# A hybrid attention and recurrence layer on one core: q and k turned by VectorE and DRAM, the recurrence's output products moved into the second score run

## The chip, the core and the metric

The kernel runs on one core of a Trainium2 chip. Five engines work from instruction queues of their own: TensorE (PE in the profile; PEld are its weight loads), VectorE (DVE), ScalarE (ACT), GpSimd (POOL) and SyncE (SP), of which the last two only issue transfers here. The metric is the device time of one execution in microseconds.

## The reference

One layer of a decoder trunk, 512 tokens, 1024 channels, all in fp32. After an RMS norm one projection gives ten groups of columns: q, k, v and a gate of an attention branch (8 heads of 64), q, f, i and g of a gated recurrence (4 heads of 128), and two merge gates.

```python
xn = rmsnorm(h, norm_gain[i])
aq, ak, av, ag, bq, bf, bi, bg, gate_a, gate_b = jnp.split(xn @ w_in[i], split_pts, axis=-1)
qa = rmsnorm(heads(aq), q_norm_gain[i]); ka = rmsnorm(heads(ak), k_norm_gain[i])
ya = moba_attention(qa, ka, heads(av), rel_bias)          # causal, with a bias by distance
ya = (ya * silu(ag)) @ w_up_a[i]
yb = hgrn2_chunkwise(silu(bq), kb, bi, log_f)             # kb and log_f come from bf
yb = (rmsnorm(yb, hgrn_out_gain[i]) * silu(bg)) @ w_up_b[i]
merged = sigmoid(gate_a) * ya + sigmoid(gate_b) * yb
h = h + merged @ w_out[i]
h = h + (p[i] @ w_ple[i]) * sigmoid(h @ w_ple_gate[i])
```

## The kernel before

Every fp32 product is made of three reduced products: each operand is split into a high part (ACT, a copy that rounds) and a low part (DVE, the difference), lines 216 to 222, and `mm3` (line 278) sums high x high, high x low and low x high. Weights come through GpSimd's queue, are split two blocks ahead of their use and held in three buffers (`wh`, `wl`). One block is 24 matmuls of 512 columns. The names of the blocks in the profile are those of the projections: `aq` and `ak` (attention's q and k, with tokens on the partitions), `av`, `bi`, and, with channels on the partitions, `bf` and `bq` (recurrence), `ag` and `bg` (silu gates), `ga` and `gb` (merge gates), `ub` and `ua` (up projections), `h`, `pe`, `g`.

The order of PE's instructions is written out: the program keeps a clock of estimated microseconds (`now`, lines 100 to 135), the projections are issued in the order of `ORDER` (line 51), and generators that stand aside (`spawn`) are resumed when that clock passes what they last yielded. So `yield 14.0` in `qk_norm`, `PACE`, `HOP` and the like say between which projections their matmuls fall. The order on ACT, DVE and SP is made by a scheduler out of its own estimates; `held` (line 143) forbids it to put an instruction ahead of the projection issued last, `held_from` (line 149) does so some microseconds of the clock later, and `tc.high_priority` moves an instruction forward. Each queue runs strictly in its order on the chip.

Four parts matter for the change.

- `qk_norm` (line 703) copies the four banks of `aq` or `ak` out of PSUM into slots of the tile `pb` (128 x 9 x 512), squares and sums them, and multiplies each head by its factor. Then it turns each pair of heads, 128 channels, on PE: four transposes of 128x128 by the identity (line 726, `qtp`, `ktp`) into one bank, from which ACT and DVE make the scaled high and low part (line 221 and 222).
- `attention` (line 734) makes for each of four head pairs two score runs: the first over queries 0 to 383 (`s` of step 0), the second over queries 384 to 511 (step 1). Behind each run stands its softmax: DVE adds a bias read from the tile `bias` (line 778), ACT exponentiates and divides (780, 782), DVE turns 32x32 blocks (785), and sixteen small transfers on SP sort the blocks (796), from slots of `pb` to other slots of `pb`. After both runs of a pair `out_values` multiplies by v (`o`, line 809).
- The recurrence (lines 493 to 700) works on one head at a time. `hgrn_intra` multiplies blocks of a 128-token chunk against each other (`lpb`, `lpa`; operands `hx`), gathers the result in one score matrix `sc` (last by ACT, line 639), and turns its keys by 32x32 blocks on DVE and through DRAM (`turned_keys`, line 599; `hkt`, `there`). `hgrn_out` makes the chunk states (`hds`, `st`) and then, `HOP` microseconds of the clock later, the output products `hop`: four of `sc` with the values and three of the states with q, into a bank of the tag `g`. ACT squares the result (667), DVE multiplies it into the gate (670), turns and sums the squares (302, 304) and so on to the normalised, gated output.
- PSUM has three banks for projections (tag `mm`), two for the recurrence (`g`), three for attention (`a`), used in turn.

Of the kernel before, what the change touches and what calls it, by code (L numbers as in the profile page):

```python
# [11 lines left out]
F32 = mybir.dt.float32  # L12
R = mybir.dt.float32r
I32 = mybir.dt.int32
AF = mybir.ActivationFunctionType
# [6 lines left out]
NT = S // 128  # L22
# [6 lines left out]
LEVELS = (16, 8, 4, 2, 1)  # L29

STEPS = ((0, 1, 2), (3,))
PACE = (20.0, 21.0)

HP = 2.5
H0 = 8.0

HOP = 9.0

BESIDE = 30.0

# [23 lines left out]
def hybrid_layer_kernel(  # L64
# [68 lines left out]
    def cost(us):  # L133
        now[0] += us
# [36 lines left out]
            xr.append(t)  # L171


    pb = cst.tile([128, 9, 512], F32, name="pb")
    xfirst = pb[:, 0, 0:272]
    raw0 = unit("w", "wf0", shape=(128, 2, 512))
    A.preload_act_table_set("natural_log_exp_and_others")
# [304 lines left out]


    hg = {}

    runs = [1000]

    def beside_attention():
        seen, until = runs[0], now[0] + BESIDE
        if seen < 1000:  # L490
            yield lambda: runs[0] > seen or now[0] >= until
# [24 lines left out]
    def hgrn_intra(h):  # L516
# [50 lines left out]
        k16 = kq(16)  # L567
        yield HP
        yield from beside_attention()
        lpb = bank("g", f"lpb{h}").rearrange("p (l c t) -> p l c t", l=4, c=NT)  # L570
        big = lpb[:, 2:4].rearrange("p l c t -> p (l c t)").rearrange("p (c t) -> p c t", c=NT)
        lpa = bank("g", f"lpa{h}").rearrange("p (l c t) -> p l c t", l=4, c=NT)
# [49 lines left out]
            yield HP  # L622
        if not h:
            kd, kts = turned_keys()
        yield 6.0 if h else 8.0

        A.activation(cum, cum, AF.Exp)
        V.tensor_tensor(q[:, 128:], q[:, 128:], cum[:, 128:], op=OP.mult)
# [13 lines left out]
    def hgrn_out(h, vb, sbg):  # L642
        kb, q, cum, kd = hg[h][:4]
        hv = slice(h * 128, h * 128 + 128)
        dsp = bank("g", f"hds{h}")
        done.add(f"hds{h}")
        for c in range(3):
            PE.matmul(dsp[:, c * 128:c * 128 + 128], kd[:, c * 128:c * 128 + 128], vb[c][:, hv],
                      start=True, stop=True)
        cost(0.65)  # L650
        st = unit("st", f"st{h}", shape=(128, 3, 128))
        V.tensor_copy(st[:, 0], dsp[:, 0:128])
        for c in (1, 2):
            e = c * 128 + 127
            V.scalar_tensor_tensor(st[:, c], st[:, c - 1], cum[:, e:e + 1], dsp[:, c * 128:c * 128 + 128],
                                   op0=OP.mult, op1=OP.add)
        yield HOP
        op_ = bank("g", f"hop{h}")
        for c in range(NT):
            s_ = slice(c * 128, c * 128 + 128)  # L660
            PE.matmul(op_[:, s_], vb[c][:, hv], sc[:, c, :], start=True, stop=(c == 0))
            if c:
                PE.matmul(op_[:, s_], st[:, c - 1], q[:, s_], start=False, stop=True)
        cost(1.5)
        o = unit("YB", f"ho{h}")
        y = unit("N", f"hy{h}")
        A.activation(o, op_, AF.Square)
        gated = f"bg{h}" in done
        if gated:
            V.scalar_tensor_tensor(sbg[h], op_, ogain[:, h:h + 1], sbg[h], op0=OP.mult, op1=OP.mult)  # L670
        token_spread(y, token_factor(token_sums(o, y, 1.0 / 128)))
        if gated:
            V.tensor_tensor(sbg[h], sbg[h], y, op=OP.mult)
        else:
            V.scalar_tensor_tensor(o, op_, ogain[:, h:h + 1], y, op0=OP.mult, op1=OP.mult)
        hg[h] += (None if gated else o,)
# [23 lines left out]
            yield HP  # L700


    def qk_norm(name, banks, g, res):
        hs = [unit("A", f"{name}h{i}", R) for i in range(HPAIRS)]
        ls = [unit("A", f"{name}l{i}", R) for i in range(HPAIRS)]
        raws = []
        ss = cst.tile([128, NT, HEADS], F32, name=name + "ss")
        y = cst.tile([128, NT, HEADS], F32, name=name + "y")
        t_ = cst.tile([128, NT, HEADS], F32, name=name + "t")
        for t in range(NT):  # L710
            raw = pb[:, (0 if name == "q" else 4) + t]
            A.activation(raw, banks[t], AF.Copy)
            sq = pb[:, ((8, 4, 5) if name == "q" else (8, 0, 1))[t % 3]]
            A.activation(sq, raw, AF.Square)
            V.tensor_reduce(ss[:, t], sq.rearrange("p (h d) -> p h d", h=HEADS), axis=AX.X, op=OP.add)
            raws.append(raw)
        V.tensor_scalar(ss, ss, 1.0 / 64, None, op0=OP.mult)
        rsqrt(y, t_, ss)
        for t in range(NT):
            r3 = raws[t].rearrange("p (h d) -> p h d", h=HEADS)  # L720
            V.tensor_tensor(r3, r3, y[:, t, :, None].to_broadcast([128, HEADS, 64]), op=OP.mult)
        yield 14.0
        for i in range(HPAIRS):
            tp = bank("a", f"{name}tp{i}")
            for t in range(NT):
                PE.transpose(tp[:, t * 128:t * 128 + 128], raws[t][:, i * 128:i * 128 + 128], ident)
            cost(0.44)
            with tc.high_priority(offset=AHEAD):
                scale_split(hs[i], ls[i], tp, g)
            res.append((hs[i], ls[i]))  # L730
            yield 1.3
        done.add(name)

    def attention(qn, kn, va, sags, res):
# [84 lines left out]

        while not {"q", "k"} <= done:  # L820
            yield lambda: {"q", "k"} <= done
        yield 3.0
        runs[0] = 0
        NS = len(STEPS)
        steps = [(hp, i) for hp in range(HPAIRS) for i in range(NS)]
# [1 line left out]
        for n in range(len(steps) + 1):  # L827
# [15 lines left out]
                    yield lambda: f"ag{ho}" in done  # L843
                out_values(ho, [pts.pop(n - NS + i_) for i_ in range(NS)])
            if n < len(steps):
                pts[n] = sorted_groups(i, softmax(hp, i, [T[hp, 0], T[hp, 1]], where))
            runs[0] += 1
        runs[0] += 1000

# [242 lines left out]
```

## Time and profile before

| | |
|---|---|
| median of 3 runs | 459.85 us (459.64 to 460.42) |
| the profiled execution, its own time | 459.45 us |
| its span, first to last instruction | 457.7 us |
| granted TensorE clock | 1.000 |
| PE busy | 451.6 us, 99% of the span |
| VectorE busy | 300.0 us, 66% |
| ScalarE busy | 276.1 us, 60% |

Rows of the chain, of a timeline and of the waits give start and length in microseconds, then engine, line, the tile written and the tiles read (`hop<-sc,biv`), and how many instructions are merged. In brackets stands how long the engine was idle before, and what ended that. A chain is followed back from the last instruction to what released each step, so what stands in it lengthens the time.

### The profile page before, as it was taken

To read this page: it belongs to the slowest core of one execution; us is meant where nothing else is said; L and a number is where in the kernel's file an instruction comes from. 1 tells how busy PE (TensorE), PEld (TensorE's weight loads), DVE (VectorE), ACT (ScalarE), POOL (GpSimd) and SP (SyncE) were. 2 spreads that over 40 slices of the span, in tenths; PEclk is the share of its full clock that TensorE was granted. 3 is DMA by queue.
4 is the path that set the end of the run, shared out by engine and by line. 5 is a ranking of instruction groups with operands and counts; after the bars stand their busy time and mean duration, and the time that the engine had idled before them with its cause. 6 is when DMAs were issued, how large, how long until landed. Compare 5 with 4: busy or idle time off the path is not lost.

```text
span 457.7 us, 8117 instructions
## 1 busy us (share of the span) xinstructions
PE 451.6 (99%) x3094; PEld 374.5 (82%) x3094; DVE 300.0 (66%) x608; ACT 276.1 (60%) x532; POOL 38.6 (8%) x77
## 2 busy tenths in 40 slices
PE   9999999999999999999999999999999999999996
PEld 8888888788888788878887888878888888888886
DVE  5869493867899586959786835564569744544222
ACT  5957565747789597968887877784435433322201
POOL 1000100000000000010100000101210100000000
PEclk9999999999999999999999999999999999999999
DMA  7802434222123626152525154454631744220111
GB/s 255 318 1 94 137 109 156 93 93 78 62 94 107 181 82 197 46 172 80 170 79 166 57 178 124 145 155 138 231 98 46 233 153 139 92 107 32 46 47 46
DMA packets 26470, 55.30 MB, mean 121 GB/s; under 512 B 6720, under 2 KB 12608, under 8 KB 26432
## 3 DMA queue, kind: packets, MB, share of 16 engines
q0 software_dynamic: 9056, 32.51, 21.7%
q1 hardware_dynamic: 17232, 22.27, 15.8%
q8 instruction: 24, 0.39, 0.4%
q14 instruction: 14, 0.11, 0.1%
q10 hardware_dynamic: 144, 0.01, 0.0%
HBM read 46.65 MB, written 2.88 MB: 108 GB/s over the span
## 4 chain that ended last, share of the span: by engine, by line
PE 96%; ACT 2%; issue 1%; DVE 1%; DVEq 0%; ACTq 0%
PE g L282 10%; PE h L282 10%; PE ga L282 9%; PE gb L282 9%; PE bf L282 5%; PE bg L282 5%; PE ub L282 5%; PE av L412 5%; PE bq L282 5%; PE ua L282 5%; PE ag L282 5%; PE bi L412 4%; PE aq L412 4%; PE ak L412 4%; PE pe L282 2%; PE o L809 2%
## 5 line engine op out<-in xcount | busy, mean ns | idle before, releaser
L217 ACT ACTIVATE wh<-wf 128x1024 fp32r<-128x1024 f32 (+1 forms) x78 | 75.6, 970 | 90.2 <-issue 32.2
L218 DVE TENSOR_TENSOR wl<-wf,wh 128x1024 fp32r<-128x1024 f32 (+1 forms) x78 | 86.8, 1112 | 53.1 <-ACT wh L217 52.8
L256 POOL DMA_DIRECT2D wf<-in_w_tr_dram x30 | 15.9, 530 | 175.2 <-DVE wl L218 135.1
L282 PE MATMUL g<-hh,wh 128*128 128x512 f32 (+1 forms) x72 | 26.3, 365 | 0.0
L282 PE MATMUL g<-hl,wh 128*128 128x512 f32 (+1 forms) x72 | 26.3, 365 | 0.0
L282 PE MATMUL g<-hh,wl 128*128 128x512 f32 (+1 forms) x72 | 26.3, 365 | 0.0
L282 PE MATMUL ga<-xh,wh 128*128 128x512 f32 x64 | 25.4, 397 | 0.0
L282 PE MATMUL gb<-xh,wh 128*128 128x512 f32 x64 | 25.0, 391 | 0.0
L282 PE MATMUL ga<-xh,wl 128*128 128x512 f32 x64 | 24.9, 390 | 0.0
L282 PE MATMUL ga<-xl,wh 128*128 128x512 f32 x64 | 24.9, 390 | 0.0
L282 PE MATMUL gb<-xh,wl 128*128 128x512 f32 x64 | 24.9, 389 | 0.0
L282 PE MATMUL gb<-xl,wh 128*128 128x512 f32 x64 | 24.9, 389 | 0.0
L282 PE MATMUL h<-mh,wh 128*128 128x512 f32 x64 | 24.9, 389 | 0.0
L282 PE MATMUL h<-ml,wh 128*128 128x512 f32 x64 | 24.9, 389 | 0.0
L282 PE MATMUL h<-mh,wl 128*128 128x512 f32 x64 | 24.9, 389 | 0.0
L780 ACT ACTIVATE pb<-pb,ps 128x128 f32<-128x128 f32 (+3 forms) x32 | 17.6, 551 | 11.0 <-DVE ps L778 10.9
L778 DVE CUSTOM_DVE_ANT_0 pb<-s,bias 128x128 f32<-128x128 f32 (+3 forms) x28 | 12.8, 497 | 11.7 <-PE s L761 8.2
L979 DVE TENSOR_TENSOR hf<-h,xres 128x512 f32<-128x512 f32 x8 | 5.5, 692 | 16.6 <-PE h L282 16.5
L782 ACT ACTIVATE pb<-pb,ps 128x128 f32<-128x128 f32 (+3 forms) x32 | 15.8, 548 | 0.0
L529 ACT ACTIVATE hx<-hx 128x512 f32<-128x512 f32 x24 | 14.8, 619 | 1.3 <-DVE hx L528 1.3
L282 PEld LDWEIGHTS g<-hh,wh 128*128 128x128 f32 x72 | 13.6, 189 | 2.2
L282 PEld LDWEIGHTS g<-hl,wh 128*128 128x128 f32 x72 | 13.6, 189 | 2.2
(345 smaller groups left out, 1247.4 us busy)
## 6 DMA issues: line engine op xcount, KB each, us to landing
wf<-in_w_tr_dram POOLq DMA_DIRECT2D x30, 512.0 KB, 3.9
wf<-in_w_tok_dram POOLq DMA_DIRECT2D x8, 512.0 KB, 3.6
wf<-in_w_up_dram POOLq DMA_DIRECT2D x16, 256.0 KB, 3.0
wf<-in_w_o_dram POOLq DMA_DIRECT2D x8, 512.0 KB, 4.1
wf<-in_w_g_dram POOLq DMA_DIRECT2D x8, 512.0 KB, 3.4
wf<-in_w_tok_dram SPq DMA_DIRECT2D x6, 512.0 KB, 7.8
pb<-pb SPq DMA_DIRECT2D x64, 48.0 KB, 2.3
bias<-in_ed_dram SPq DMA_DIRECT2D x8, 256.0 KB, 4.3
```

The costliest lines, as they stand in the source:

```text
L217: A.activation(hi, src, AF.Copy)
L218: V.tensor_tensor(lo, src, hi.bitcast(F32), op=OP.subtract)
L256: (G if len(wraw) >= FAR else nc.sync).dma_start(raw, ap)
L282: dense.append(PE.matmul(ps, a[:, k, :], b[k], start=(n == 0), stop=(n == tot - 1)))
L412: dense.append(PE.matmul(banks[t], a[:, s_], b[:, kk, :], start=(k == 0 and i == 0), stop=(k == KD - 1 and i == 2)))
L529: A.activation(x, x, AF.Exp)
L778: in_order(V.tensor_tensor_reduce(p_, s_[:, so:so + nk], T[j][:, nk - 1::-1], -1.0, 3e38, OP.add, OP.min, st[:, 0:1]))
L780: A.activation(p_, p_, AF.Exp, bias=st[:, 0:1], scale=-1.0, accum_out=st[:, 1:2])
L782: A.activation(p_, p_, AF.Copy, scale=st[:, 2:3])
L809: PE.matmul(o[64 * j:64 * j + 64, qs], va[kb][:, h0:h0 + 64], pt[:, :, 4 * b_ + o0 // 128 + kb, :], start=(kb == 0), stop=(kb == qb))
L979: V.tensor_tensor(t, ps, xres, op=OP.add)
```

## The change

q is no longer turned on PE at all, and of k only the first head pair. Instead DVE turns the 32x32 blocks of the normalised tiles into free slots of `pb` (line 745 of the changed kernel), SP writes them to DRAM and reads them back with the blocks in order (lines 747 and 768), and ACT and DVE make the high and low parts from there (`split_pairs`, lines 754 and 755). q's splits are issued when k has been normalised, and held seven microseconds of the clock past that; the splits of k's pairs 1 to 3 are issued with the first run's softmax and held 16, 18 and 20 microseconds past it. `pb` has a tenth slot. The output products of heads 0 to 2 are put into a list, and the next head's `hgrn_intra` issues them right ahead of its `lpb`, where the second score run stands; they take a bank of the tag `mm`.

```diff
-PACE = (20.0, 21.0)
+PACE = (21.0, 21.0)
-HOP = 9.0
+HOP = 10.0
-    pb = cst.tile([128, 9, 512], F32, name="pb")
+    pb = cst.tile([128, 10, 512], F32, name="pb")
@@ hgrn_intra
         yield from beside_attention()
+        while hops:
+            hops.pop()()
         lpb = bank("g", f"lpb{h}").rearrange("p (l c t) -> p l c t", l=4, c=NT)
...
-        yield 6.0 if h else 8.0
+        yield 4.0 if h else 8.0
@@ hgrn_out
-        yield HOP
-        op_ = bank("g", f"hop{h}")
-        for c in range(NT):
-            s_ = slice(c * 128, c * 128 + 128)
-            PE.matmul(op_[:, s_], vb[c][:, hv], sc[:, c, :], start=True, stop=(c == 0))
-            if c:
-                PE.matmul(op_[:, s_], st[:, c - 1], q[:, s_], start=False, stop=True)
-        cost(1.5)
+        op_ = []
+
+        def products():
+            op_.append(bank("mm", f"hop{h}"))
+            for c in range(NT):
+                s_ = slice(c * 128, c * 128 + 128)
+                PE.matmul(op_[0][:, s_], vb[c][:, hv], sc[:, c, :], start=True, stop=(c == 0))
+                if c:
+                    PE.matmul(op_[0][:, s_], st[:, c - 1], q[:, s_], start=False, stop=True)
+            cost(1.5)
+
+        if h < GH - 1:
+            hops.append(products)
+            yield lambda: op_
+        else:
+            yield HOP
+            products()
+        op_ = op_[0]
@@ qk_norm
-            A.activation(raw, banks[t], AF.Copy)
-            sq = pb[:, ((8, 4, 5) if name == "q" else (8, 0, 1))[t % 3]]
+            with tc.high_priority(offset=AHEAD):
+                A.activation(raw, banks[t], AF.Copy)
+            sq = pb[:, 8 + t % 2]
...
-        yield 14.0
-        for i in range(HPAIRS):
-            tp = bank("a", f"{name}tp{i}")
+        if others:
+            parts.clear()
+            others.pop()()
+            held_from(7.0, list(parts))
+        z0, d0 = (4, 0) if name == "q" else (0, 6)
+        there = scratch.tile([128, NT, 512], F32, tag="there", name=f"{name}there")
+        for t in range(NT):
+            V.transpose(pb[:, z0 + t].rearrange("p (b i c) -> p b i c", b=4, c=32),
+                        raws[t].rearrange("p (i b c) -> p b i c", b=4, c=32))
+            nc.sync.dma_start(there[:, t], pb[:, z0 + t])
+        turned = pb[:, d0:d0 + 4].rearrange("p s f -> p (s f)")
+
+        def split_pairs(i0):
+            for i in range(i0, HPAIRS):
+                tp = turned.rearrange("p (u i c) -> p i u c", i=HPAIRS, c=32)[:, i]
+                h_, l_ = (u[i].rearrange("p (u c) -> p u c", c=32) for u in (hs, ls))
+                parts.append(held(A.activation(h_, tp, AF.Copy, scale=g)))
+                V.scalar_tensor_tensor(l_, tp, g, h_.bitcast(F32), op0=OP.mult, op1=OP.subtract)
+                res.append((hs[i], ls[i]))
+
+        if name == "k":
+            yield 15.0
+            tp = bank("a", "ktp")
             for t in range(NT):
-                PE.transpose(tp[:, t * 128:t * 128 + 128], raws[t][:, i * 128:i * 128 + 128], ident)
+                PE.transpose(tp[:, t * 128:t * 128 + 128], raws[t][:, 0:128], ident)
             cost(0.44)
             with tc.high_priority(offset=AHEAD):
-                scale_split(hs[i], ls[i], tp, g)
-            res.append((hs[i], ls[i]))
-            yield 1.3
+                scale_split(hs[0], ls[0], tp, g)
+            res.append((hs[0], ls[0]))
+        for b in range(4):
+            nc.sync.dma_start(turned[32 * b:32 * b + 32].rearrange("k (t g f) -> k t g f", g=4, t=NT),
+                              there.rearrange("(g k) t (b f) -> b k t g f", g=4, b=4)[b])
+        others.append(lambda: split_pairs(0 if name == "q" else 1))
+        yield 2.0
         done.add(name)
@@ attention
-        yield 3.0
+        yield 5.0
...
-                pts[n] = sorted_groups(i, softmax(hp, i, [T[hp, 0], T[hp, 1]], where))
+                z = softmax(hp, i, [T[hp, 0], T[hp, 1]], where)
+                if others:
+                    parts.clear()
+                    others.pop()()
+                    for n_, p_ in enumerate(list(parts)):
+                        held_from(16.0 + 2.0 * n_, [p_])
+                pts[n] = sorted_groups(i, z)
```

On PE, before the change, head 1's products stand inside the block gb3, nine projections after its start; `sc` is the score matrix, `biv` the values, `st` the states, `ha1` the head's q:

```order
L282 MATMUL gb3_2156<-xh2_428,wl31_1895 128x512
L661 MATMUL hop1_2166<-sc_93,biv0_393 128x128 x2
L663 MATMUL hop1_2166<-ha1_1372,st1_2078 128x128
L661 MATMUL hop1_2166<-sc_93,biv2_396 128x128
L663 MATMUL hop1_2166<-ha1_1372,st1_2078 128x128
L661 MATMUL hop1_2166<-sc_93,biv2_396 128x128
L663 MATMUL hop1_2166<-ha1_1372,st1_2078 128x128
L282 MATMUL gb3_2156<-xh3_436,wh31_1894 128x512
```

On PE, after the change, they follow the last scores of head pair 1's second run (`s110`, `s111`) and stand ahead of head 2's `lpb2`, inside the block bq3:

```order
L801 MATMUL s110_2226<-kl1_1135,qh1_878 128x512
L801 MATMUL s111_2227<-kl1_1135,qh1_878 128x512
L666 MATMUL hop1_2262<-sc_93,biv0_393 128x128 x2
L668 MATMUL hop1_2262<-ha1_1316,st1_2069 128x128
L666 MATMUL hop1_2262<-sc_93,biv2_396 128x128
L668 MATMUL hop1_2262<-ha1_1316,st1_2069 128x128
L666 MATMUL hop1_2262<-sc_93,biv2_396 128x128
L668 MATMUL hop1_2262<-ha1_1316,st1_2069 128x128
L580 MATMUL lpb2_2270<-hx2_64_2083 32x64 x8
L585 MATMUL lpb2_2270<-hx2_32_2113 32x32 x8
L551 MATMUL lpb2_2270<-ha2_1774,hk2_1783 32x32 x16
```

The products moved by some two blocks of projections, and the second run with the next head's `lpb` now falls into bq, where it fell into bf.

On DVE, before the change, these rows led up to the second transpose of the same run's probabilities (line 785); `ps` are the softmax's sums, `wl35` a weight split:

```order
L781 RECIPROCAL ps130_2268<-ps130_2268 128x1
L587 TENSOR_TENSOR s322_2091<-lpb2_2296,mkf_69 128x128
L781 RECIPROCAL ps131_2274<-ps131_2274 128x1
L530 TENSOR_TENSOR hx2_8_2413<-hk2_1798,hx2_8_2413 128x32x8
L535 TENSOR_TENSOR hx2_8_2413<-ha2_1789,hx2_8_2413 128x32x8
L218 TENSOR_TENSOR wl35_2376<-wf35_2373,wh35_2375 128x1024
L785 STREAM_TRANSPOSE pb_70<-pb_70 128x4x128
L499 TENSOR_SCALAR hu3_2426<-bf3_2238 128x512
L527 TENSOR_TENSOR hx2_4_2459<-hu2_1793 128x64x4
L527 TENSOR_TENSOR hx2_2_2477<-hu2_1793 128x128x2
L528 TENSOR_TENSOR hx2_2_2477<-hu2_1793 128x128x2
L785 STREAM_TRANSPOSE pb_70<-pb_70 128x4x128
```

On DVE, after the change, these do (the transposes are line 825 now); `hop1` is read at L683, `hk3` is head 3's gate out of bf:

```order
L529 TENSOR_TENSOR hx2_4_2459<-hu2_1778 128x64x4
L505 TENSOR_TENSOR hk3_2416<-ha3_2407,bf3_2188 128x512
L683 SCALAR_TENSOR_TENSOR bg1s_1467<-hop1_2262,sm_68,bg1s_1467 128x512
L302 STREAM_TRANSPOSE hy1_2345<-ho1_2344 128x512
L590 TENSOR_TENSOR s322_2082<-lpb2_2270,mkf_69 128x128
L528 TENSOR_TENSOR hx2_2_2488<-hu2_1778 128x128x2
L529 TENSOR_TENSOR hx2_2_2488<-hu2_1778 128x128x2
L825 STREAM_TRANSPOSE pb_70<-pb_70 128x4x128
L531 TENSOR_TENSOR hx2_8_2441<-hk2_1783,hx2_8_2441 128x32x8
L536 TENSOR_TENSOR hx2_8_2441<-ha2_1774,hx2_8_2441 128x32x8
L507 TENSOR_TENSOR ha3_2407<-ha3_2407,hu3_2411 128x512
L825 STREAM_TRANSPOSE pb_70<-pb_70 128x4x128
```

The gates of head 3 and two steps of the products' way to the output moved in front of the transposes, and a weight split moved away. For head 0 and pair 0 the order is the same but for L304 and one more multiplication ahead of the second transpose.

On SP, after the change, the transfers of q and k stand between the recurrence's first keys and the bias tables of head pair 0 (`bias00`, `bias01`), which before the change followed those keys directly:

```order
L613 DMA hkt0there_978<-hkt0_976 128x384
L615 DMA hkt0_976<-hkt0there_978 32x4x96 x4
L747 DMA qthere_911<-pb_70 128x512 x4
L768 DMA pb_70<-qthere_911 32x16x128 x4
L747 DMA kthere_1172<-pb_70 128x512 x4
L768 DMA pb_70<-kthere_1172 32x16x128 x4
L876 DMA bias00_1360<-in_ed_dram 128x512
L876 DMA bias01_1362<-in_ed_dram 128x512
L613 DMA hkt1there_1762<-hkt1_1760 128x384
```

More of the change, by code (lines that the diff above doesn't have):

```diff
@@ L484, in hybrid_layer_kernel @@
     hg = {}
+    hops = []
     runs = [1000]
@@ L700, in recurrence @@
             yield HP
+    others, parts = [], []
     def qk_norm(name, banks, g, res):
```

## The prediction

> **What bounds the kernel now.** I read the head of the page first, then the chain of waits in order of time, then TensorE's waits, and for the work that the change hands over the timelines of VectorE and SyncE.
>
> ```profile
> span 457.7 us, 8117 instructions
> PE 451.6 (99%) x3094; PEld 374.5 (82%) x3094; DVE 300.0 (66%) x608; ACT 276.1 (60%) x532; POOL 38.6 (8%) x77
> ```
>
> TensorE (PE) is busy for 451.6 of 457.7 us. So time is won in two ways alone: by instructions that leave PE, and by waits of PE that go. The chain (start, length, what, how many) shows the price of both:
>
> ```profile
> 32.28 16.32 PE av L412 x72
> ...
> 98.43 0.44 PE qtp L726 x4
> 98.87 1.40 PE ak L412 x6
> ...
> 111.60 0.44 PE hop L661 x4
> ...
> 113.16 2.77 PE bg L282 x12
> ...
> 124.10 0.44 PE ktp L726 x4
> 124.53 1.40 PE bf L282 x6
> ...
> 129.60 0.44 PE ktp L726 x4
> 130.04 4.13 PE bq L282 x18
> 134.17 0.68 PE bg L282 x3
> 134.85 0.65 PE s L761 x7
> ...
> 146.68 5.44 PE gb L282 x24
> ...
> 157.78 0.36 PE lpb L577 x16
> ...
> 159.47 0.90 PE bf L282 x3
> ...
> 193.03 0.94 issue
> ...
> 197.69 3.44 PE gb L282 x15
> ...
> 205.88 0.90 PE s L761 x6
> ...
> 230.17 2.33 PE o L809 x40
> ...
> 241.69 0.95 issue
> ...
> 246.34 8.19 PE ga L282 x36
> ```
>
> A projection matmul costs 16.32 / 72 = 0.2267 us. Groups of four transposes (qtp, ktp) stand between projections, and at 193.03 and 241.69 the chain leaves PE. PE's own rows there name the wait:
>
> ```profile
> 195.86 0.71 PE L661 MATMUL hop<-sc,biv 128*128 128x128 f32 x4 [0.62 <-ACT sc L639]
> 244.51 0.71 PE L661 MATMUL hop<-sc,biv 128*128 128x128 f32 x4 [0.61 <-ACT sc L639]
> ```
>
> The output products of heads 1 and 2 (hop) are reached before ScalarE (ACT) has written the last blocks of the score matrix sc. Those of head 0, from 111.60 to 113.16, wait for nothing: 1.56 us is their bare price.
>
> **Part by part.** *Transposes that leave PE.* A group takes 0.44, and the six projections behind it 1.40 where six cost 1.36: 0.48 with the slower restart, 0.44 where something else follows. Before the change there are eight groups; all of q's and three of k's go. Seven at 0.44 to 0.48 are 3.1 to 3.4 us; from 124.10 to 130.04, 5.94 less 18 projections (4.08), k's four cost 1.86, or 0.465 each, so I take 7 x 0.465 = 3.25. On PE nothing comes in their place.
>
> One transpose lasts longer than its share of a group:
>
> ```profile
> L726 PE MATMUL qtp<-ident,pb x16: 270/272/273, 98.3 to 104.5; 128*128 128x128 f32 x16
> ```
>
> 0.272 us is its duration, but four fit in 0.44, since they overlap; the place in the chain is the price. The Trainium skill (TensorE: Matmul & The Clock Gate, Part 4: PE-mode transpose) puts a 128x128 transpose inside a kernel at about 275 ns. The row's duration agrees, and a sum by that figure would remove 28 x 0.275 = 7.7 us and end at 450.1; I keep to the chain.
>
> *The products of heads 0 to 2.* They move behind the six score matmuls of the second run, ahead of the next head's lpb, and their 1.56 us are paid there too. What goes is the wait. From 193.03 to 197.69 are 4.66 us; nine projections (24 less the 15 behind) take 2.04 and hop 1.56, so 1.06 is lost. From 241.69 to 246.34 likewise 4.65 - 2.04 - 1.56 = 1.05. At the new place (205.88 in the old times) sc has been ready for ten microseconds, so 2.1 us go. Head 3 stays.
>
> *q's way through DRAM.* Its rows, of VectorE (DVE), of SyncE's queue (SP) and of transfers (size, microseconds from issue to landing):
>
> ```profile
> 92.17 2.50 DVE L721 TENSOR_TENSOR pb<-pb,qy 128x512 f32<-128x512 f32 x4
> ...
> 114.47 2.46 DVE L721 TENSOR_TENSOR pb<-pb,ky 128x512 f32<-128x512 f32 x4
> ...
> 146.62 1.89 DVE L785 STREAM_TRANSPOSE pb<-pb 128x512 f32<-128x512 f32 x3
> ```
>
> ```profile
> 68.60 1.75 SPq L612 DMA_DIRECT2D hkt<-hkt0there  x4
> 70.39 0.91 SPq L836 DMA_DIRECT2D bias<-in_ed_dram  x2
> ```
>
> ```profile
> bias<-in_ed_dram SPq DMA_DIRECT2D x8, 256.0 KB, 4.3
> pb<-pb SPq DMA_DIRECT2D x64, 32.0 KB, 2.2
> ...
> out_dram<-sg SPq DMA_DIRECT2D x7, 256.0 KB, 2.0
> ...
> hkt<-hkt0there SPq DMA_DIRECT2D x4, 48.0 KB, 1.9
> ```
>
> q is normalised by 94.7. Four DVE transposes at 1.89 / 3 = 0.63 end at 97.2, the writes land 2.0 later, at 99.2. Four transfers back are issued in 1.75 and land between 1.9 (the blocks of 48 KB) and 4.3 us behind (256 KB, their size): by 105. ACT's order has q's splits behind k's square roots, near 111, and the first scores come near 131 (134.85 less 3.25 and hop's 1.56, plus six projections of bg): covered. k's copies out of PSUM must now wait until q's writes have read the same slots of pb, 97 to 99, about when ak's first banks end: nothing. The 5 us that DVE turns for q and k lie where it waits for weights anyway, and hop's followers of head 0 leave that stretch.
>
> *k's way.* k is normalised at 116.9, now 1.8 earlier, for q's groups are gone. A weight split, two of q's splits and a gate product (estimates of 0.6 to 1.2 each) come before its transposes: end near 121, written by 123. The transfers back wait for pair 0's transposes on PE too, near 123.5, and land by 130. The bias tables of pair 0, issued at 70 before, stand behind them on SP: issued near 126, landed near 130.5. The first scores end near 132.8, and DVE reaches them near 134.7: two to four microseconds to spare. Pairs 1 to 3 are wanted 45 us later.
>
> *The first run's sorted tiles.* Their transfers overwrite the slots that k's pairs 1 to 3 are split from, and those splits are held past gb (152.12 less 3.25 and 1.56: 147.3). With a weight split, a sigmoid step and two splits before the last, they start near 151.5, six microseconds after the tiles are ready. One run costs SP:
>
> ```profile
> 214.97 10.79 SPq L796 DMA_DIRECT2D pb<-pb  x16
> 225.81 1.18 SPq L836 DMA_DIRECT2D bias<-in_ed_dram  x2
> ```
>
> They end near 162.3; the second run's transposes, which overwrite their source, come near 164. Nothing is lost, and little is spare.
>
> *The second run.* Two of hop's followers (L670, L302), and for pair 0 a third (L304), now come on DVE ahead of the second transpose of the probabilities, which stood here (below it, the group of the weight splits, 1223 ns each):
>
> ```profile
> 214.24 0.70 DVE L785 STREAM_TRANSPOSE pb<-pb 128x512 f32<-128x512 f32 x1
> ```
>
> ```profile
> L218 DVE TENSOR_TENSOR wl<-wf,wh 128x1024 fp32r<-128x1024 f32 x62 | 75.8, 1223 | 50.9 <-ACT wh L217 50.6
> ```
>
> It ended at 214.94, SP's sixteen at 225.76, and 2.2 later, at 228.0, the last tile had landed. o began at 230.17 and reads these tiles in the last 16 of its 40 matmuls, from 231.6: 3.6 us to spare. In the new order four more steps of 512 elements stand before that transpose (gates of the next head among them) and a weight split less: 4 x 0.63 - 1.2 = 1.3 us; for pair 0 a reduction and a multiplication more, another 1.3. The distance from scores to o falls by 0.3 (from 24.3 to 24.0: scores 0.90, hop 1.56, lpb and lpa 1.69, 81 projections 18.4, the next scores near 1.46). That leaves 2.0 us for pair 1 and 0.7 for pair 0. I take the cost as nothing; its upper end is 3 us for both. A PSUM bank binds too: gb takes bf's bank one block sooner, 9.6 us after bf's end (24 projections 5.44, scores 0.90, hop 1.56, the next head's lpb and lpa 1.69, from 157.78 to 159.47), but by DVE's order bf has been read out some 7 us after it: covered.
>
> *Below nothing.* One more PE wait might vanish, ak's for q's last copy:
>
> ```profile
> 87.25 0.50 PE L412 MATMUL ak<-wh,xh 128*128 128x512 f32 x1 [0.33 <-ACT pb L712]
> ```
>
> The copy has a higher priority now, yet stands at the same place of ACT's order; I count 0, with 0.6 (0.33 and the slower restart) as the range's end.
>
> **Sum.** 3.25 + 2.1 = 5.35 us. Of the profiled execution's 459.45 that leaves 454.1; the median of the runs, 459.85, lies 0.4 above that execution, so **454.5**.
>
> **Rivals.** *The second run is too full.* The sixteen transfers land after o wants them, for pairs 0 and 1, or bf's bank is late. For it: 0.7 and 2.0 us are less than the error of my sums. Against: o's first 24 matmuls don't need them, and pair 2, with no gates of a next head, has more room. With 1 to 3 us given back it ends at 455.5 to 457.5, say 456.4.
>
> *Only the transposes pay.* The products wait at the new place too, for the bank that they now take from the projections. Against it: that bank's last reader, the first step of a sigmoid on ACT, belongs to a projection that ended more than six microseconds before. Then 459.85 - 3.25 = 456.6.
>
> *The way back is slow, and the kernel slower than before.* ACT stands at q's first split from near 111 on, and behind it in its order is the weight of the second head's bq, which PE reaches near 124. The splits of that weight and of q need 4 to 5 us, so q may land as late as 119, 20 us after its issue; from there each microsecond is lost on PE, and after 25 the gain is used up. If landing grew with the number of pieces (hkt's 128 rows of 384 bytes in 1.9; here four times 512 rows of 512 bytes, 16 times as many), it would be 30 us: 454.5 + 10 = 464.5. Against: hkt goes the same way, in whole runs of bytes, in 1.9. The Trainium skill (VectorE: DVE Perf Modes, The three transpose paths) warns that a plain copy that transposes by its access pattern is 19 times slower than the crossbar's where the destination's innermost stride is large. Here DVE turns the 32x32 blocks and the copies move runs of 512 bytes, so its condition isn't met; no run here shows such a copy.
>
> **How the numbers follow.** The forecast has 0.70, the full second run 0.19, the transposes alone 0.05, the slow way back 0.06. The low end is the forecast less 0.6 and some of the runs' spread (0.4): 453.5. The high end, 457.0, takes in most of the full second run and the transposes alone; the slow way back is left out. A measurement of this kernel can tell about 0.2%, 0.9 us, from no change: all but the last rival are faster by more, and a way back that eats just the gain gives the 0.02 within it; 0.06 stay for slower, with a jam that I haven't seen.
>
> **What would show it.** In the changed profile: one group ktp and none of qtp in the chain; hop three times right behind six s, without a wait for sc; PE's busy time down by 3 us or more. The forecast is wrong if PE waits at o for pb (the second run was too full), at gb for DVE's reading of bf (the bank), at hop for the bank, or at bq or bg near 112 to 130 for a weight (the way back).

## The result and the profile after

The changed kernel takes 456.07 us (median of 6 runs, 455.39 to 457.09); the kernel before took 460.15 beside it (459.64 to 460.62). The ratio is 0.9915, with a 95% interval of 0.9901 to 0.9928: 0.85% less, about 4 us of the 5.35 in the forecast. The profiled execution took 455.39 us, with a span of 453.6 where before had 457.7. Its head:

```profile
span 453.6 us, 8108 instructions
PE 448.7 (99%) x3066; PEld 372.3 (82%) x3066; DVE 303.1 (67%) x616; ACT 276.5 (61%) x532; POOL 38.4 (8%) x77
```

PE has 28 instructions and 2.9 us of busy time less. The chain of waits answers to the one of before: one group ktp and none of qtp, the first scores at 131.48 (the forecast said near 131), and no place where hop is waited for. New in it is a stretch ahead of o of pair 1 that leaves PE for the sorting transfers on SP:

```profile
123.51 0.44 PE ktp L762 x4
...
131.48 0.65 PE s L801 x7
...
154.29 0.94 PE s L801 x6
...
223.46 0.59 SPq L836
224.05 0.04 issue
224.10 3.88 DMA bias<-in_ed_dram
227.98 0.06 issue
228.04 1.09 PE o L849 x16
...
351.55 43.52 PE h L282 x192
```

The profile names a bias table as what ended o's wait, but o reads no table. What o reads are the sorted tiles. The last of them landed at 227.59, 0.45 us before o went on at 228.04; in mixed (below) the last tile landed at 230.32, o went on at 230.81, and the table landed at 231.67 only.

h begins at 351.55; before it began at 355.65, 4.1 us later. PE's own list of waits has only the one for ak that before had too, and warm's. So what is missing from the forecast isn't one large wait. The starts of PE's instructions show it, stage by stage. They need a kernel between the two, the one called products_room below: the products moved as in the change, q and k on PE. All three have the same number of projections between these starts (us between first starts, from PE's timelines):

| from, to | before | products_room | after |
|---|---|---|---|
| first bf, first scores of pair 1 | 131.59 | 131.40 | 128.38 |
| of these, first bf to first scores of all | | 86.09 | 82.85 |
| scores of pair 1, of pair 2 | 48.66 | 47.94 | 48.07 |
| scores of pair 2, of pair 3 | 48.65 | 47.93 | 48.23 |
| scores of pair 3, first h | 78.15 | 78.15 | 78.15 |
| sum | 307.05 | 305.42 | 302.83 |

The sum fell by 4.22; ahead of the first bf the profiled execution after was 0.12 slower (48.56 for 48.44), where nothing is changed. The ends of the row that prices the transposes, first of after, then of products_room (start, length, what):

```profile
48.56 0.39 PE L282 MATMUL bf<-xh,wh 128*128 128x512 f32 x1
...
131.41 0.33 PE L801 MATMUL s<-kh,qh 64*128 64x128 f32 x2
```

```profile
48.32 0.39 PE L282 MATMUL bf<-xh,wh 128*128 128x512 f32 x1
...
134.41 0.33 PE L774 MATMUL s<-kh,qh 64*128 64x128 f32 x2
```

From start to start these are 82.85 and 86.09 us: seven groups of transposes are worth 3.24 us. The products are worth 307.05 - 305.42 = 1.63, and 0.65 is lost again in the score runs.

What the products cost now shows around 203, where hop stands behind scores; the second fence is the same group of before, between projections:

```profile
203.00 0.40 PE L801 MATMUL s<-kl,qh 64*128 64x512 f32 x2
203.33 0.71 PE L666 MATMUL hop<-sc,biv 128*128 128x128 f32 x4
...
205.09 0.43 PE L580 MATMUL lpb<-hx 128*32 128x64 f32 x16
```

```profile
111.44 0.60 PE L661 MATMUL hop<-sc,biv 128*128 128x128 f32 x4
...
112.92 0.48 PE L282 MATMUL bg<-xh,wh 128*128 128x512 f32 x1
113.23 0.40 PE L282 MATMUL bg<-xl,wh 128*128 128x512 f32 x1
```

Behind scores the group takes 1.76 (203.33 to 205.09). Between projections it takes 1.48, and the next projection but one starts 0.08 late (0.31 for 0.23): 1.57. Between scores and lpb it costs 0.2 more.

Two transfers landed late. The copies of q and k back into SBUF (size of each, median us from issue to landing), and DVE at the first scores:

```profile
pb<-qthere SPq DMA_DIRECT2D x4, 256.0 KB, 7.5
...
pb<-kthere SPq DMA_DIRECT2D x4, 256.0 KB, 6.2
```

```profile
135.49 0.29 DVE L818 CUSTOM_DVE_ANT_0 pb<-s,bias 128x128 f32<-128x128 f32 x1 [0.34 <-DMA bias<-in_ed_dram]
```

The second bias table of pair 0, behind k's copies on SP, landed at 135.4, where the forecast had 130.5, and DVE waited for it.

### The profile page after: what moved, and what is told of

It reads as the page before. It is cut to its first block, busy times and chain, and to the rows that moved or that the text cites. A ratio compares the mean times of both kernels' runs of the same rounds, so it can differ in the third digit from the quotient of the medians.

```text
span 453.6 us, 8108 instructions
## 1 busy us (share of the span) xinstructions
PE 448.7 (99%) x3066; PEld 372.3 (82%) x3066; DVE 303.1 (67%) x616; ACT 276.5 (61%) x532; POOL 38.4 (8%) x77
## 4 chain that ended last, share of the span: by engine, by line
PE 81%; DVE 7%; SPq 4%; DMA 3%; ACT 2%; issue 2%; DVEq 0%; ACTq 0%
PE g L282 10%; PE ga L282 10%; PE h L282 10%; PE ub L282 5%; PE ua L282 5%; PE av L412 5%; PE bi L412 5%; PE aq L412 4%; SPq L836 4%; PE ak L412 4%; PE gb L282 4%; PE bf L282 4%; PE ag L282 4%; PE bg L282 3%; PE bq L282 3%; PE pe L282 2%
## 5 line engine op out<-in xcount | busy, mean ns | idle before, releaser
L256 POOL DMA_DIRECT2D wf<-in_w_tr_dram x30 | 15.8, 528 | 171.1 <-DVE wl L218 109.7
```

The lines of the kernel that those rows point to most:

```text
L256: (G if len(wraw) >= FAR else nc.sync).dma_start(raw, ap)
```

## The experiments

Twelve kernels, each beside runs of before of its own. "Price" in the expectations is my theory after the result: the wait was smaller than the chain says, and the products cost more behind scores. Its first rival, "transfers", puts the missing part down to the added transfers; later ones are told as they come.

**The products alone (products_alone).** The kernel before with the products moved, two of the change's delays (kd at 4.0, HOP 10), and PACE as before:

```diff
+        def products():
+            op_.append(bank("mm", f"hop{h}"))
...
+        if h < GH - 1:
+            hops.append(products)
+            yield lambda: op_
```

> The kernel before with the move of the products alone: q and all of k stay with the transposes on PE. The sum on record: 2.1 us less than before (ratio 0.9954), for the two waits for sc of 1.05 each. Theory of the price: from start to start the waits were only about 0.9 each (193.03 to 200.96 is 7.93 us, less 24 projections 5.44, less the bare 1.57 from 111.44 to 113.23 less one projection), and behind scores the products cost 1.76 where they cost 1.57 between projections, 0.2 three times: about 1.2 us less (ratio 0.9974). Theory of the transfers (what is missing was lost to the added transfers): 2.1 us less, since no transfer is added here.

459.85 us beside 460.03, ratio 0.9997 (0.9984 to 1.001): nothing, where I had 1.2 or 2.1. The waits for sc are gone, but PE has two others, at o of pair 1:

```profile
228.97 1.53 PE L822 MATMUL o<-pb,avv 128*64 128x128 f32 x24 [0.46 <-ACT sgb L287]
231.16 1.09 PE L822 MATMUL o<-pb,avv 128*64 128x128 f32 x16 [0.66 <-DMA pb<-pb]
```

o waits for its bank, and then for the last sorted tiles (the last landed at 230.71). DVE's last transpose of the probabilities started 13.8 us after the second run's scores (218.22 and 204.43); before it was 8.4 (214.24 and 205.81). This is the rival of the full second run, and here it eats everything.

**The products alone, with room (products_room).** One number more of the change:

```diff
-PACE = (20.0, 21.0)
+PACE = (21.0, 21.0)
```

> The products alone, as run before, with one number more taken from the change: one us more between the first and the second run's scores (PACE 21 for 20). There o of pair 1 took 3.22 us where 2.33 is bare, and the scores ahead of it 0.53 more for a bank. If the shortage of the move lies in that second run (the last transposes of the probabilities came 14.5 us behind the scores, 9.1 before the change), a second run that starts one us later against its blocks has head 3's gates half a block later on DVE, and o's wait falls: 0.5 to 1.2 us less than before, ratio 0.9975 to 0.999. If the place of the scores makes no difference, the time is again that of before, 1.000.

457.77 us beside 459.7, ratio 0.9964 (0.9951 to 0.9977): 1.7 us less, more than I expected. PE has no wait left but warm's and ak's. The second run's scores now stand six projections into bq and no longer at its head, and DVE gets to the transposes sooner: the sixteen transfers start 10.2 us after the scores (215.3 and 205.06), in products_alone 14.5 (218.96 and 204.43). So the PACE that the diff carries with it is no trimming; without it the move is worth nothing.

**The turning alone (turn_alone).** The changed kernel with the products as before, HOP 9:

```diff
-        if h < GH - 1:
-            hops.append(products)
...
+        yield HOP
+        op_ = bank("g", f"hop{h}")
```

> The changed kernel with the products back at their own place between projections, on their old bank: the turning of q and k alone. The sum on record and the theory of the price: 3.25 us less than before (ratio 0.9929), and hop of heads 1 and 2 waits for sc again, 0.6 each in PE's rows. Theory of the transfers: only about 2.0 less (ratio 0.9957), with PE waits or slower starts in places where before had none.

469.69 us beside 460.03, ratio 1.0208 (1.0188 to 1.0228): 9.7 us slower than before, against every theory I had. PE's waits:

```profile
PE bg L282 <- DVE ps L808: 5.7, 1, 5.7
PE hop L664 <- ACT sc L642: 4.0, 2, 3.4
PE gb L282 <- DVE ha L514: 1.1, 1, 1.1
```

DVE's rows there show why (two of the softmax, one of head 1's gates):

```profile
136.83 0.29 DVE L808 CUSTOM_DVE_ANT_0 pb<-s,bias 128x128 f32<-128x128 f32 x1 [2.84 <-DMA bias<-in_ed_dram]
...
137.88 0.42 DVE L808 CUSTOM_DVE_ANT_0 pb<-s00x,bias 128x256 f32<-128x256 f32 x1
...
139.18 0.69 DVE L500 TENSOR_SCALAR hu<-bf 128x512 f32<-128x512 f32 x1
```

In the changed kernel head 1's gates (hu from bf) come at 125.55, ahead of the first softmax. Here what follows head 0's products on ACT and DVE lies between 113 and 134, among k's norm, q's splits and the transposes, and the gates fall behind the softmax, to 139.18. They hold the banks of bf and bq, so bg, which begins right behind the scores, gets (by the time of its release, 138.37) the bank of the scores' extra tile (`s00x`, which has a bank of the tag `mm`) and stands until DVE has read it; and that reading waited 2.84 for a table. From here the gates' followers are late too: the keys of head 1 go out at 151.77, in the changed kernel at 134.93. About 3.7 of the 9.7 us are not the waits but what follows them: behind the waits at bg and at hop the granted clock falls to 0.50 for a while (the last section), and PE's work there takes 1.9 and 1.8 us longer.

**Later products (products_later).** The turning alone with HOP 11.

```diff
-HOP = 9.0
+HOP = 11.0
```

> As the turning alone, but the products come two us later (HOP 11 for 9), between projections and after sc is ready, not behind scores. Theory of the price: no wait for sc is left, the products cost 1.57 and not 1.76, the second run keeps its old room so that o of pair 1 doesn't start late: 3.25 + 1.8 = 5.05 us less than before, 454.8 where the changed kernel has about 456 (ratio to before 0.989). The sum on record: 5.35 less, as it gave for the changed kernel. Theory of the transfers: no better than the changed kernel, 4.1 less (0.991).

465.21 us, ratio 1.0106 (1.0091 to 1.0122). Head 0's products are still in that stretch: bg waits 3.7 for DVE, hop of head 2 still 0.9 for sc. It doesn't tell the price; it shows that two us of delay give back 4.5.

**One us more behind the second run (second_run_wider).**

```diff
-PACE = (21.0, 21.0)
+PACE = (21.0, 22.0)
```

> The changed kernel with one us more between a second run's scores and the next (PACE 21, 22). Theory of the price: o of pair 1, 2.65 us in the changed kernel where 2.33 is bare, loses its 0.3 of waiting: 0.3 us less than the changed kernel, 4.4 less than before (0.9905). If o's 2.65 is not a wait for the transfers, nothing changes there and the time is that of the changed kernel (0.991).

457.27 us, ratio 0.9937 (0.9921 to 0.9952), 1.2 more than the changed kernel. o's own 2.65 did fall to 2.34, so it was a wait; but now o waits for its bank, whose turn has come round to one that is still read:

```profile
PE o L849 <- DVE bg3s L479: 1.5, 1, 1.5
```

**Head 0 alone put back (head0_back).** From here the question is why the turning alone is slow. The theories: the place of head 0's products ("order") or the late tables ("tables").

```diff
-        if h < GH - 1:
+        if 0 < h < GH - 1:
             hops.append(products)
...
-            yield HOP
+            yield HOP if h else 9.0
```

> The changed kernel with head 0's products alone back at their old place, near 112, on their old bank; heads 1 and 2 stay behind the second run's scores. The turning alone was 9.7 us slower than before, and PE waited 5.7 us there at bg1 for DVE's reading of a bank. Theory of the order: head 0's products and what follows them on ACT and DVE stand ahead of head 1's gates in the stretch that q and k now fill; the gates fall behind the softmax of the first scores, and the bank of bf1 that they read is late. Then PE waits 4 to 7 us at bg1 again, and this kernel is slower than the changed one by 5 or more: 461 or above. If it is heads 1 and 2 whose move makes the gain, this kernel stays within 1 us of the changed one, 456 to 457.

Head 0's products are on their old bank here too. 463.5 us beside 459.8, ratio 1.0084 (1.0067 to 1.0101), 7.4 more than the changed kernel, as the order has it (1.7 of them is the lower clock behind the wait at bg, whose 24 projections take 7.15 us for 5.44):

```profile
PE bg L282 <- DVE ps L818: 5.4, 1, 5.4
PE gb L282 <- DVE ha L514: 1.2, 1, 1.2
```

The tables have a share in it here too: DVE, with no gates ahead of the softmax, waits 2.00 and 0.72 us for them.

**Heads 1 and 2 in their own turn (mixed).** Head 0 moved, the others at 12 us after hds, on their old bank:

```diff
-        if h < GH - 1:
+        if h == 0:
             hops.append(products)
...
-            yield HOP
+            yield 12.0 if h < GH - 1 else HOP
```

> The changed kernel with head 0's products behind the second run's scores as there, but those of heads 1 and 2 in their own turn between projections, 12 us after hds, two us later than before the change. Theory of the price: no wait for sc, 1.57 and not 1.76 for each, o of pair 1 not late (2.33 and not 2.65): 0.6 to 0.9 us less than the changed kernel, about 455.3, ratio to before 0.9895. Sum on record (products behind scores cost what they cost between projections, and are covered there): the same as the changed kernel, 456.1, 0.991.

458.95 us, ratio 0.9982 (0.997 to 0.9993): 2.9 more than the changed kernel, where I had 0.8 less.

```profile
PE ga L282 <- DVE ps L818: 1.3, 1, 1.3
PE hop L666 <- ACT sc L642: 1.1, 2, 0.9
PE o L849 <- DMA bias<-in_ed_dram: 0.9, 1, 0.9
```

sc is ready later than before the change: in the changed kernel ACT's last copies into it run from 194.38 to 195.6, 14 us behind hds (181.64); before it was 11 (184.73 to 195.8). A product "in its own turn" still meets it, and o of pair 1 (for its sorted tiles) and a bank of ga are late as well. So the move of heads 1 and 2 is worth more than its waits, and my idea that they would stand better between projections is wrong, at 12 us at least.

**The tables early, in the changed kernel (bias_early) and with the turning alone (turn_bias_early).** In both, pair 0's tables are issued behind q's copies and ahead of k's:

```diff
+        bias(0)
         while not {"q", "k"} <= done:
...
-                if i == 0:
-                    for j in range(2):
...
+                if i == 0 and n:
+                    bias(hp)
```

> The changed kernel with the bias tables of pair 0 issued ahead of k's transfers (after q's) and not behind them. In the changed kernel DVE waited 0.34 us for the second of them, at 135.5, where the forecast had 130.5. Theory of the order: DVE's wait goes, PE has no wait there anyway: same as the changed kernel within 0.3, ratio to before 0.990 to 0.9925. If the late tables hold back what follows (hx of head 1, first sorted tiles), it is 0.3 to 1 us less.

456.06 us, ratio 0.9919 (0.9901 to 0.9938): the same, as expected. In its profile DVE waits for no table and gb and bf lose nothing, but o of pair 1 takes 3.09 us, 0.44 more than in the changed kernel's:

```profile
229.22 1.09 PE L849 MATMUL o<-pb,avv 128*64 128x128 f32 x16 [0.54 <-DMA pb<-pb]
```

> The turning of q and k alone, as run before, with the bias tables of pair 0 issued ahead of k's transfers. There DVE waited 2.84 us for a table, and PE 5.7 at bg1. Theory of the tables (they alone make the turning slow): PE's 5.7 goes, and with it most of the loss: 3 us less than before, ratio 0.993. Theory of the order: the 2.84 go, but head 1's gates still stand behind the softmax: PE's wait at bg1 falls to about 3, hop still waits for sc, and the kernel is still slower than before: ratio 1.01 to 1.016.

467.3 us, ratio 1.0161 (1.0144 to 1.0178), 2.4 less than the turning alone, PE's wait at bg down from 5.7:

```profile
PE hop L664 <- ACT sc L642: 3.3, 2, 2.7
PE bg L282 <- DVE ps L808: 2.5, 1, 2.5
PE gb L282 <- DVE ha L514: 1.4, 1, 1.4
```

The tables make up three of the 5.7; the rest is put down to the order. The ratio lies a hair above the expected range.

The changed kernel's runs spread over 1.7 us, those of before over 1.0. The tables' landing can be a part of that. In six executions with the turning and head 0's products moved (k0_too, whose scores come late, is left out): us from the first scores to DVE's second step on them, and what the 48 projections of gb and bf, 10 us later, took beyond 10.88:

| kernel | DVE's second step after the scores | gb and bf beyond 10.88 |
|---|---|---|
| bias_early | 3.60 | 0.00 |
| after | 4.08 | 0.09 |
| mixed | 4.19 | 0.18 |
| second_run_wider | 4.39 | 0.42 |
| two_queues | 4.54 | 0.57 |
| two_queues_012 | 4.99 | 0.99 |

In these six, each 0.1 us of lateness past 4.0 is 0.1 us of PE's: bf takes the bank that bg's last step on DVE (L479) reads, and that step stands behind the softmax. In PE's weight loads of after:

```profile
147.18 0.19 PEld L282 LDWEIGHTS bf<-xh,wh 128*128 128x128 f32 x1 [0.21 <-DVE bg1s L479]
```

It isn't the whole: the runs of bias_early, where no table is late, spread over 2.7 us (454.98 to 457.63), and o of pair 1 varies from profile to profile as well (2.65, 3.09 and 3.48 us in after, bias_early and mixed). The worst of the six for the tables, of two_queues_012, in DVE's row:

```profile
136.51 0.29 DVE L818 CUSTOM_DVE_ANT_0 pb<-s,bias 128x128 f32<-128x128 f32 x1 [0.85 <-DMA bias<-in_ed_dram]
```

**Two queues (two_queues), and for pairs 0 to 2 alone (two_queues_012).** G is GpSimd; the second kernel has "step and hp < HPAIRS - 1 and a > 1" as its condition.

```diff
-    nc.sync.dma_start(pt[32 * b:32 * b + 32, a], z[32 * a:32 * a + 32, b])
+    (G if step and a > 1 else nc.sync).dma_start(pt[32 * b:32 * b + 32, a], z[32 * a:32 * a + 32, b])
```

> The changed kernel with half of a second run's sixteen transfers issued by GpSimd's queue and half by SP's. SP takes 10.8 us for sixteen, and o of pair 1 waited 0.31 in the changed kernel for the last of them. If that serial issue is what holds o: the wait goes, 0.3 less than the changed kernel, 455.7, ratio to before 0.9905, and no wait at o in any run. If the transposes ahead of it on DVE or the landing hold it, nothing changes: 456.1. If weights behind these transfers on GpSimd's queue come late, it is slower by as much as PE then waits for a weight: 457 or more.

456.76 us beside 459.7, ratio 0.9928 (0.9915 to 0.9942). o of pair 1 is at its bare 2.33, but ub now waits for weights behind these transfers, the third of the three ways (456.76 where it had 457 or more):

```profile
PE ub L282 <- ACT wh L217: 0.3, 1, 0.3
...
PE ub L282 <- DVE wl L218: 0.3, 1, 0.3
```

> The two queues again, but for pairs 0 to 2 alone: the second run of pair 3 keeps all its transfers on SP. With two queues in every second run, o of pair 1 took its bare 2.33 us and the tables of the next pair were issued by 219.3 where the changed kernel had 225.2, but the weights of ub, queued behind the transfers of pair 3 on GpSimd's queue, came late and cost about 1.2 us. Theory: without that, the 0.3 of o stays gained and nothing is lost: 302.5 us from the first bf to the first h where the changed kernel has 302.83 and all of before's waits are gone; 455.7, ratio to before 0.9905, which a measurement can't tell from the changed kernel's 0.9915. If weights come late in the other runs too, 456.5 or more.

455.35 us beside 460.23, ratio 0.9901 (0.9883 to 0.9918). No o waits and ub doesn't; this profile's one new wait is that of bf behind the late table. It is the fastest kernel of the study, but its interval covers the changed kernel's: it isn't shown to be better. With the tables early as well it wasn't tried. The landing of a second run's sixteen transfers, of after on SP alone and then of two_queues_012 on both queues:

```profile
DMA to landing us min/median/max: 1.8/2.7/5.0
```

```profile
DMA to landing us min/median/max: 1.7/1.8/2.2
```

SP issues eight in 4.95 us where sixteen took 10. In after the first eight landed within 1.9 us of their issue and the last eight took 3.4 to 5.0, with two weight loads of 512 KB, issued at 218.75 and 221.29, in flight beside them. The Trainium skill (DMA: Bandwidth & Descriptors, Issuing engines are not separate DMA queues) says that starting transfers on several engines only saves the time to initiate them, usually small beside the transfer. Here it isn't small: sixteen take 10 us to issue, and each 1.8 to 5.0 to land.

**Pair 0 of k through DRAM too (k0_too).**

```diff
-            tp = bank("a", "ktp")
-            for t in range(NT):
-                PE.transpose(tp[:, t * 128:t * 128 + 128], raws[t][:, 0:128], ident)
...
+                split_pairs(0, 1)
```

> The changed kernel with pair 0 of k through DRAM as well, so that no transpose of q or k stays on PE. By the price of the sum on record a group of four is worth 0.465 us: 455.6, ratio to before 0.990, if k's way back has room for it. k's transfers back were issued from 124.0 to 126.7 and landed 3.4 (median) to 8.2 us later, and the first scores came at 131.4: if the last of them lands after 129, PE waits for pair 0's split and the gain is eaten: 456 to 459. The forecast's own landing time (130) makes that a loss of one to two us, since the split of 1.4 us still follows.

462.55 us beside 459.7, ratio 1.0062 (1.0046 to 1.0079), 6.5 more than the changed kernel and 3.5 above the expectation's worst case. PE stands at the first scores until k's last copy is there and split:

```profile
PE s L796 <- ACT kh L754: 4.5, 1, 4.5
```

```profile
134.68 0.72 ACT L754 ACTIVATE kh<-pb,sm 128x512 fp32r<-128x512 f32 x1 [4.86 <-DMA pb<-kthere]
```

k's copies, issued from 123.6 to 126.2, are all there at 134.6. (The 3.4 us in the expectation is the median of k's writes and reads together; the four reads alone have 6.2.) Of the 6.5, PE's wait makes 4.5, less the 0.46 of the group. Nearly all of the rest is the clock: it is at 0.50 from 134.87 to 141.70, just when PE goes on, and PE's work there takes 2.9 us longer (the third figure from the end is the clock):

```profile
134.90:141.60 6.70, 6.05 (x26) 4.75 (x27) 5.31 (x19) 5.09 (x14) 0.00 (x0) 0.50 0.28 106
```

## Why the prediction was right, and where it was not

The sign, the two sources and the range (453.5 to 457.0) held. By its time alone 456.07 lies nearer to the rivals (456.4 for the full second run, 456.6 for the transposes alone) than to the 454.5 of the forecast; it is the stages that tell them apart. Of the forecast's signs, PE's busy time fell by 2.9 us where 3 or more was asked, and one sign of being wrong, PE waiting at o for pb, did appear, with 0.32 us. Point by point:

- *Transposes, 3.25.* Measured 3.24. The place in the chain was the price, 0.463 a group. The Trainium skill's 275 ns (TensorE: Matmul & The Clock Gate, Part 4: PE-mode transpose) is the duration of one again; an estimate by it, 28 times, would have been 7.7.
- *The products, 2.1.* Measured 1.63; this is the mis-sized term. 1.06 for each wait was read from the chain's start at 197.69, which lies 0.25 behind the start that PE's timeline of before has for the same projections:

```profile
197.44 0.48 PE L282 MATMUL gb<-xh,wh 128*128 128x512 f32 x1
```

  From start to start, 193.03 to 200.96 are 7.93; less 24 projections (5.44) and the bare 1.57, 0.92 were lost. And "their 1.56 us are paid there too" doesn't hold: 1.76 are. That leaves 0.73 for each of two heads, and the table shows 0.72 and 0.72. Head 0's move, which had no wait to lose, gives 0.19 though its price is 0.2: the lpb and lpa of head 1 right behind take 1.36 us in products_room (159.78 to 161.14) and took 1.69 before (157.71 to 159.40). Why they were slower there is open, and neither the forecast nor the later price had it.
- *The second run, cost nothing.* o of pair 1 lost 0.32 and pair 0 nothing, where I had 2.0 and 0.7 to spare. SP ended at 224.05, and the last tiles landed 3.4 to 5.0 us after issue, where the forecast had 2.2 for all. This is the rival "too full" in small; products_alone shows it in full, and that PACE keeps it small.
- *k's way and the tables.* Back "by 130" and tables at 130.5 "with two to four microseconds to spare" were wrong: 134.2 and 135.4. k's pairs 1 to 3 aren't split until 147.45, so that cost nothing; the tables cost 0.09 at bf in this execution and up to 1 in those of other kernels. I took the landing from lone transfers of other stretches. Here the DMA engines are full: in k0_too their share from 130.6 to 135.4 is 1.03.
- *q's way.* Issued until 102.7, the last of its copies landed at 109.7; I had 105. The first split stood at 110.68 and waited for nothing: covered, but by less than a microsecond.
- *The rest* held: gb and hop found their banks, and the first run's tiles started at 152.24 (forecast 151.5).

So 5.35 forecast, less 0.47 for the products and 0.65 in the score runs (0.32 at o, the rest at bf and lpb), is 4.23; 4.22 was measured.

What the prediction missed altogether isn't in its sum. It added the two halves as if each stood alone. Measured apart they are +9.7 us (the turning) and 0, or -1.7 with PACE (the products). That head 0's followers leave the stretch where q and k are turned was one clause about DVE's time; in fact the turning depends on it, as head0_back shows: 7.4 us. Part of that is the place of the scores, which in turn_alone and head0_back fall right ahead of bg and so find no free bank behind them; how much of the 7.4 is that, how much the late gates and how much the tables, the runs don't tell (in turn_alone, early tables give back 2.4). That the transposes paid what the sum gave them was in this respect luck.

## What to carry to other kernels

Where a change has several edits, ask of each what it would cost without the others: here the edit that looked like a small gain (head 0's products) was the one that made room for the large one. Read the length of a wait from start to start on the waiting engine, less the bare work from the same kind of row, not from the chain's merged pieces. And price a moved group of instructions by its new neighbours, and a transfer's landing by what is in flight beside it.

## What the runs showed of the hardware

*A short wait costs twice.* In turn_bias_early PE waited 2.5 us at bg, behind ten small matmuls of the scores. The table by windows has the stretch of the wait, the one behind it, and then the latter in two parts (length, busy time of PE, PEld, DVE, ACT and POOL, then the granted clock, the DMA share and GB/s):

```profile
132.40:135.50 3.10, 0.66 (x10) 0.34 (x6) 2.95 (x11) 1.52 (x7) 0.53 (x1) 1.00 0.81 194
135.50:142.70 7.20, 7.16 (x24) 5.78 (x25) 6.16 (x20) 6.42 (x18) 0.00 (x0) 0.76 0.20 73
136.20:139.50 3.30, 3.30 (x10) 2.56 (x9) 2.42 (x11) 3.30 (x12) 0.00 (x0) 0.50 0.26 102
139.60:142.70 3.10, 3.10 (x15) 2.55 (x14) 3.04 (x7) 2.32 (x4) 0.00 (x0) 1.00 0.02 5
```

Behind the wait the clock is 0.76 in the mean of 7.2 us: 0.50 from 136.16 to 139.57, then 1.00 again. bg's 24 projections take 7.21 where 5.44 is usual: 1.77 us more, on top of the 2.5. Between 10 and 440 us of all fourteen traces the clock is either 1.00 or 0.50. It was 0.50 for 3.41 us behind PE's waits of 2.5, 2.7 and 3.4 us (the last two at hop in turn_bias_early and turn_alone), for 6.83 us behind those of 3.7, 4.5, 5.4 and 5.7, and never behind one of 1.5 or less. The Trainium skill (TensorE: Matmul & The Clock Gate, Part 1: The HAM clock gate) gives an idle window of about 3.4 us as what lowers the clock. Here the wait was 2.5, in a stretch of 3.1 us in which PE was busy for 0.66: a stretch that isn't wholly idle was enough.

*Weights aren't loaded ahead behind scores.* Between projections the load of hop's first weights starts 0.22 us before its matmul (111.22 and 111.44), while the projection still runs; behind the scores, whose operands fill 64 rows, it starts with it, after 0.37 us of nothing:

```profile
203.32 0.52 PEld L666 LDWEIGHTS hop<-sc,biv 128*128 128x128 f32 x4 [0.37 <-issue]
```

That is the likely source of most of the 0.2 us; whether it is the 64 rows or something else in the scores, no run tells.
